# Order of attends, gating products and first loads in a hybrid attention encoder layer

## The chip, the cores and the metric

One core of a Trainium2 chip runs the whole layer. The metric is the device time of one execution in microseconds (us), from the first instruction to the last. The engines are named as the profile names them: PE is TensorE's matrix products and PEld its weight loads, DVE is VectorE, ACT is ScalarE, POOL is GpSimd, SP is SyncE, whose queue issues most of the loads.

## The reference

1024 tokens of width 1024 pass one layer: an attention mixer of four heads and a spatial gating mixer of four groups side by side, an output projection, and an MLP of width 4096, which the change doesn't touch. Cut to the mixers:

```python
h = rmsnorm(x, norm_mix_g)
q, k, v, g, a_f, a_b, su, sv = split(h @ w_in)
# attention, per head, 16 chunks n of 64 tokens, forward scan and mirrored backward scan
b = cumsum(log_a, within the chunk)
scores = mask(q*exp(b - b_mid) @ (k*exp(b_mid - b)).T)
kv[n] = (k*exp(b_last - b)).T @ v
s[n+1] = exp(b_last)[n] * s[n] + kv[n]
o = scores @ v + (q*exp(b)) @ s[n]
o = rmsnorm(o_fwd + o_bwd) * gla_norm_g * silu(g)
# spatial gating, per group of 128 channels, 8 chunks of 128 tokens
v = rmsnorm(gelu(sv)) * sgu_norm_g
out = gelu(su) * (w_s @ v + b_s)
x = x + concat([attention, gating]) @ w_out
x = x + square(relu(rmsnorm(x) @ w1)) @ w2
```

## The kernel before, in words

**Products.** Every operand of a large product is split into a high part (a cast on ACT, L124) and a low part (the difference, on DVE, L125), and each product is three matmuls: high by high, high by low, low by high, all at L106 in `mm`. They add up in PSUM banks: four of the kind `pf` for the projections and four of the kind `pg`, taken in turn, for everything small. A product that takes a bank waits until what was in it has been read.

**The start.** ACT's queue loads the first half of the input's first block, SP's queue the first block of the weights of V (L182, a tile `wr`), then the 24 column vectors of norms (L183, `cols`, 12 KB), then the rest of the inputs `xT` (L194) and the weights `wv` (L135). ACT scales the input by a column of `cols` into `xa` (L186), DVE makes its low part `xb` (L187), and casts (L185) and subtracts (L190) the first weights. The V projection then runs over eight blocks of K, 24 matmuls each.

**The stream.** `stream` (L554) yields 64 steps. Each step is some twelve matmuls of a projection (q, k, attention gate, gating u) or a part of the gating's v. Between the steps lie small pieces of attention and gating, listed in `ev` by hand with the step after which each is issued (L570 to L583). PE executes in the order in which the program is written (`mm` and `transp` keep it, L103 to L110); the other engines' order is set by the scheduler of the framework.

**The pieces.** `u = 2h + hf` numbers head h and half hf of the tokens. For each there are `gate` (decay logarithms `la`, L338), `st_cum` (sums over the chunk, L359), `st_score` (scores and masked copies into `P`, L391, L403), `st_tr` (transposition `kd`, L408) and `st_kv` (L416). `st_kv` fills the states `X[h]`, 16 slots of 128. Its lower 64 partitions are the forward scan, upward from slot 1 (L438). The upper 64 are the backward scan, which runs only when both halves are there, from slot 14 down to slot 0: 14 steps at L444, each of which reads the slot above it. `st_attend` (L449) adds up, in one bank, four products of V and P and eight of X and `qd`: half hf reads the slots 8 hf to 8 hf + 7. Its squares go through ACT (L466), POOL (L211, L212) and DVE (L468). `st_out` (L471) transposes the result, and DVE multiplies it by a column of `cols` and by the head's gate (L476), which the projection of step 39 or 40 (27, 28; 51, 52; 63, 64) leaves.

**Spatial gating.** `sgu_v(hf)` makes one half's v, which POOL scales at its end (L517). `sgu_mix(hf, g)` (L522) is one set of four products for half hf and group g, in a bank that DVE evacuates into `SV` (L526). The names in the trace are `pg<-k,V` for such a set, since `cws` and `cbs` lie in buffers of kind k and SV in one of kind V, and `pg<-V,P`, `pg<-X,qd` and `pg<-ident,kd` for an attend's two parts and a transposition.

The lines that the change and the prediction turn on:

```python
b1 = 7 + 6 * (2 * h + 1) + 11
ev.append((b1 + hf, st_attend, h, hf))
ev.append((b1 + 4 + hf, st_out, h, hf))
```

`b1` is 24, 36, 48 and 60 for the four heads.

Of the kernel before, what the change touches and what calls it, by code (L numbers as in the profile page):

```python
# [31 lines left out]
def tile_encoder(  # L32
# [25 lines left out]
    nc = tc.nc  # L58
# [6 lines left out]
    def sb(tag, bufs, shape=(P, 512), dt=F32):  # L65
        cnt[0] += 1
        home = tiny if tag in ("sm", "rso", "r3") else pool
        return home.tile(list(shape), dt, tag=tag, bufs=bufs, name=f"{tag}{cnt[0]}")

    def one(name, shape, dt=F32):  # L70
        return tiny.tile(list(shape), dt, tag=name, bufs=1, name=name)
# [7 lines left out]
    def in_table_order(ins):  # L79

        if table["last"] is not None:
            tc.add_manual_dep(
                ins.ins,
                table["last"].ins.name,
                mybir.DependencyInfo(mybir.DependencyClass.NoSync, mybir.DependencyReason.DATA),
                reason="table order",
            )
        table["last"] = ins
# [11 lines left out]
    def pg():  # L100
        return bank("pg")

    def mm(o, lhsT, rhs, start, stop, more=False):  # L103

        tc.keep_in_program_order(
            nc.tensor.matmul(out=o, lhsT=lhsT, rhs=rhs, start=start, stop=stop, skip_group_check=more)  # L106
        )
# [4 lines left out]
    def v3(ap, a):  # L112
        return ap.rearrange("p (a b) -> p a b", a=a)

    def bcast_in(ap, n):
        return ap[:, None, :].broadcast_to([ap.shape[0], n, ap.shape[1]])
# [5 lines left out]
    def split(src, hi, lo, scale=None):  # L122
        if scale is None:
            nc.scalar.copy(out=hi, in_=src)  # L124
            return nc.vector.tensor_tensor(out=lo, in0=src, in1=hi.bitcast(F32), op=ALU.subtract)  # L125
        else:
            nc.scalar.activation(out=hi, in_=src, func=AF.Copy, scale=scale)
            nc.vector.scalar_tensor_tensor(
                out=lo, in0=src, scalar=scale, in1=hi.bitcast(F32), op0=ALU.mult, op1=ALU.subtract
            )  # L130

    def wpiece(src):
        with tc.high_priority(offset=HP):
            raw = sb("wr", 2)
            nc.sync.dma_start(out=raw, in_=src)  # L135
            hi, lo = sb("wh", 3, dt=F32R), sb("wl", 3, dt=F32R)
            split(raw, hi, lo)
        return hi, lo
# [3 lines left out]
    ccols = one("cols", [P, 24])  # L142
# [12 lines left out]
    def in_order(ins, after):  # L155
        if after is not None:
            tc.add_manual_dep(
                ins.ins,
                after.ins.name,
                mybir.DependencyInfo(mybir.DependencyClass.NoSync, mybir.DependencyReason.DATA),  # L160
                reason="order of use",
            )
        return ins

    for k in range(KT):
        for hf in range(2):
            raw = sb("qk", 8)
            a, b = sb("xa", 16, dt=F32R), sb("xb", 16, dt=F32R)
            g = ccols[:, G1 + k : G1 + k + 1]
            xh[k, hf], xl[k, hf] = a, b  # L170
            if k == 0 and hf == 0:
                wraw = sb("wr", 2)
                whi, wlo = sb("wh", 3, dt=F32R), sb("wl", 3, dt=F32R)
                h0, h1 = slice(0, 256), slice(256, 512)
                with tc.high_priority(offset=1000):
                    first = nc.scalar.dma_start(out=raw[:, h0], in_=xT[0, :, h0])
                    table["last"] = in_order(
                        nc.scalar.preload_act_table_set("natural_log_exp_and_others"), first
                    )
                    table["logexp"] = True  # L180
                    in_table_order(nc.scalar.copy(out=one("wact", [P, 8]), in_=warm[:, 0:8]))
                    lead = nc.sync.dma_start(out=wraw, in_=wv[0])  # L182
                    lead = in_order(nc.sync.dma_start(out=ccols, in_=cols), lead)  # L183
                    lead = in_order(nc.sync.dma_start(out=raw[:, h1], in_=xT[0, :, h1]), lead)
                nc.vector.tensor_copy(out=whi, in_=wraw)  # L185
                in_table_order(nc.scalar.activation(out=a[:, h0], in_=raw[:, h0], func=AF.Copy, scale=g))  # L186
                nc.vector.scalar_tensor_tensor(  # L187
                    out=b[:, h0], in0=raw[:, h0], scalar=g, in1=a[:, h0].bitcast(F32), op0=ALU.mult, op1=ALU.subtract
                )
                nc.vector.tensor_tensor(out=wlo, in0=wraw, in1=whi.bitcast(F32), op=ALU.subtract)  # L190
                split(raw[:, h1], a[:, h1], b[:, h1], g)
                wvp.append((whi, wlo))
            else:
                nc.sync.dma_start(out=raw, in_=xT[k, :, hf * 512 : hf * 512 + 512])  # L194
                split(raw, a, b, g)
                if hf == 0:
                    wvp.append(wpiece(wv[k]))
# [324 lines left out]
    def sgu_mix(hf, g):  # L522
        mx = pg()
        for i in range(4):
            mm(mx[:, i * P : i * P + P], SV[:, hf * 4 + i, g, :], cws[:, g * P : g * P + P], True, True)
        nc.vector.scalar_tensor_tensor(  # L526
            out=SV[:, hf * 4 : hf * 4 + 4, g, :], in0=v3(mx, 4), scalar=ccols[:, GS + g : GS + g + 1],
            in1=bcast_in(cbs[:, g * P : g * P + P], 4), op0=ALU.mult, op1=ALU.add,
        )
# [40 lines left out]
    ev = []  # L570
    for h in range(H):
        for hf in range(2):
            u = 2 * h + hf
            b0 = 7 + 6 * u
            for off, fn in ((-3 if u == 2 else -4, gate), (0, st_cum), (4, st_score), (5, st_tr), (7, st_kv)):
                ev.append((b0 + off, fn, h, hf))
            b1 = 7 + 6 * (2 * h + 1) + 11
            ev.append((b1 + hf, st_attend, h, hf))
            ev.append((b1 + 4 + hf, st_out, h, hf))
    for g in range(4):  # L580
        ev.append((21 + g, lambda hf, g: sgu_mix(hf, g), 0, g))
        ev.append((41 + g, lambda hf, g: sgu_mix(hf, g), 1, g))
    ev.sort(key=lambda e: e[0])  # L583
    pos = 0
    for _ in stream():
        pos += 1
        while ev and ev[0][0] <= pos:
            _, fn, h, hf = ev.pop(0)
# [553 lines left out]
```

## Time and profile before

| | |
|---|---|
| Runs shown | 1019.97, 1015.92, 1019.59 us; median 1019.59 |
| The profiled execution | 1017.8 us, its span 1016.0 us |
| Granted PE clock, mean | 0.995 |
| Busy | PE 98%, DVE 68%, ACT 47%, POOL 9% |
| Chain that ended last | PE 92%, DVE 5%, ACT 1%, DMA 1% |
| Read from memory, written | 106.77 MB, 37.75 MB |

The profile is one execution. A busy share is that of the whole span; a row of the timeline has the start of an instruction, or of a few alike in a row, their time together, and in brackets the idle time of the engine before them and who ended it. The granted clock is a share of PE's full speed. The stream of 64 steps with attention and gating lies between about 50 and 310 us; what follows is the output projection and the MLP.

### The profile page before, as it was taken

Reading aid. Unit: us, or ns where it says so; the run is one execution under the profiler, and the core shown is the slowest. Engines: PE = TensorE matmul, PEld = TensorE weight load, DVE = VectorE, ACT = ScalarE, POOL = GpSimd, SP = SyncE. Lnnn points to the kernel's source line nnn. Section 1 sums busy time; section 2 is a strip of 40 time slices with the busy share of each in tenths; the row PEclk is TensorE's granted clock in tenths of the full one; section 3 lists DMA queues with packets and bytes.
Section 4 is the critical chain, followed back from the end, with each engine's and each line's share of the span. In section 5 each row is a group of like instructions: output and inputs, shape, how many; then the busy total and the mean of one; then the engine's idle time right before and its main releaser. Section 6 shows DMA issues by size and latency. Waiting matters only on the chain.

```text
span 1016.0 us, 14249 instructions
## 1 busy us (share of the span) xinstructions
PE 1000.5 (98%) x5014; PEld 825.1 (81%) x5014; DVE 693.0 (68%) x1178; ACT 474.0 (47%) x887; POOL 92.6 (9%) x101
## 2 busy tenths in 40 slices
PE   9999999898999999999999999999999999999997
PEld 7887888787888888888888888887888888788885
DVE  6245877776684557877677677665446776799684
ACT  6634646664464446434444433333444444445463
POOL 1001521342220000000000000000000000004031
PEclk9999999999999999999999999999999999999999
DMA  9422111110113444646446445226975652367342
GB/s 307 163 72 74 42 33 63 42 38 26 54 42 123 136 125 134 208 155 218 146 176 214 150 154 177 104 96 232 362 264 178 206 193 69 111 246 263 104 145 83
DMA packets 84984, 145.46 MB, mean 143 GB/s; under 512 B 8881, under 2 KB 17841, under 8 KB 84913
## 3 DMA queue, kind: packets, MB, share of 16 engines
q1 hardware_dynamic: 83760, 142.59, 41.8%
q10 hardware_dynamic: 1152, 1.97, 0.5%
q8 instruction: 39, 0.64, 0.3%
q14 instruction: 33, 0.26, 0.1%
HBM read 106.77 MB, written 37.75 MB: 142 GB/s over the span
## 4 chain that ended last, share of the span: by engine, by line
PE 92%; DVE 5%; ACT 1%; DMA 1%; issue 1%; SPq 0%; POOL 0%; POOLq 0%; DVEq 0%; ACTq 0%
PE pf L106 64%; PE pg L106 27%; PE pg L110 1%; DVE X L444 1%; DVE wl L125 1%; DVE X L438 1%; DMA k<-w 0%; DVE P L403 0%; DMA cols<-cols 0%; DMA wr<-wsv 0%; DVE qk L329 0%; DVE la L343 0%; DVE wl L628 0%; ACT wh L124 0%; DVE kin L382 0%
## 5 line engine op out<-in xcount | busy, mean ns | idle before, releaser
L106 PE MATMUL pg<-xa,xa 128*128 128x512 f32 x768 | 182.5, 390 | 0.4 <-DVE wh L628 0.2
L106 PEld LDWEIGHTS pg<-xa,xa 128*128 128x128 f32 x768 | 144.1, 188 | 31.0 <-DVE wh L628 0.7
L106 PE MATMUL pf<-xa,xa 128*128 128x512 f32 x576 | 138.8, 390 | 0.4 <-ACT kn L792 0.4
L106 PE MATMUL pf<-xa,wh 128*128 128x512 f32 x336 | 136.0, 405 | 0.0
L106 PE MATMUL pf<-xb,wh 128*128 128x512 f32 x336 | 131.9, 392 | 0.0
L106 PEld LDWEIGHTS pf<-xa,xa 128*128 128x128 f32 x576 | 108.0, 188 | 23.3 <-ACT kn L792 0.8
L106 PE MATMUL pf<-xa,wl 128*128 128x512 f32 x320 | 125.6, 393 | 0.0
L124 ACT CAST xa<-xb 128x512 fp32r<-128x512 f32 x76 | 47.1, 621 | 98.2 <-PE pf L106 74.8
L106 PE MATMUL pf<-V,xa 128*128 128x512 f32 x336 | 91.7, 389 | 0.0
L125 DVE TENSOR_TENSOR xa<-xb,xa 128x512 fp32r<-128x512 f32 x76 | 52.3, 689 | 52.8 <-ACT xa L124 52.6
L125 DVE TENSOR_TENSOR wl<-wr,wh 128x512 fp32r<-128x512 f32 x63 | 49.9, 793 | 50.1 <-ACT wh L124 49.8
L106 PEld LDWEIGHTS pf<-xa,wh 128*128 128x128 f32 x336 | 63.9, 190 | 13.9 <-issue 1.2
L941 POOL TENSOR_SCALAR r<-r 128x1 f32<-128x1 f32 x8 | 14.9, 1868 | 657.5 <-ACT tmp L939 657.3
L106 PEld LDWEIGHTS pf<-V,xa 128*128 128x128 f32 x336 | 63.1, 188 | 13.1
L106 PEld LDWEIGHTS pf<-xb,wh 128*128 128x128 f32 x336 | 63.8, 190 | 11.9
L106 PEld LDWEIGHTS pf<-xa,wl 128*128 128x128 f32 x320 | 60.5, 189 | 13.0
L124 ACT CAST wh<-wr 128x512 fp32r<-128x512 f32 x63 | 38.7, 615 | 63.6 <-PE pf L106 54.1
L124 ACT CAST xa<-k 128x512 fp32r<-128x512 f32 x49 | 30.5, 623 | 68.4 <-PE pf L106 66.4
L106 PE MATMUL pf<-xb,xa 128*128 128x512 f32 x192 | 53.9, 389 | 0.0
L106 PE MATMUL pf<-qk,xa 128*128 128x512 f32 x176 | 52.9, 390 | 0.0
L124 ACT CAST xa<-la 128x512 fp32r<-128x512 f32 x34 | 21.1, 622 | 46.5 <-PE pf L106 27.5
L106 PEld LDWEIGHTS pf<-xb,xa 128*128 128x128 f32 x192 | 36.1, 188 | 7.4
(296 smaller groups left out, 1840.4 us busy)
## 6 DMA issues: line engine op xcount, KB each, us to landing
k<-w SPq DMA_DIRECT2D x64, 256.0 KB, 3.1
hA<-kn SPq DMA_DIRECT2D x32, 256.0 KB, 3.1
hS<-wr SPq DMA_DIRECT2D x32, 256.0 KB, 4.3
la<-hA SPq DMA_DIRECT2D x17, 256.0 KB, 5.1
la<-hS SPq DMA_DIRECT2D x17, 256.0 KB, 2.7
qk<-xn SPq DMA_DIRECT2D x16, 256.0 KB, 5.5
wr<-wsv SPq DMA_DIRECT2D x16, 256.0 KB, 2.6
wr<-wo SPq DMA_DIRECT2D x16, 256.0 KB, 2.6
```

Of the source, the lines that this page charges most:

```text
L106: nc.tensor.matmul(out=o, lhsT=lhsT, rhs=rhs, start=start, stop=stop, skip_group_check=more)
L110: tc.keep_in_program_order(nc.tensor.transpose(out=o, in_=i, identity=cid))
L124: nc.scalar.copy(out=hi, in_=src)
L125: return nc.vector.tensor_tensor(out=lo, in0=src, in1=hi.bitcast(F32), op=ALU.subtract)
L438: nc.vector.scalar_tensor_tensor(out=x[lo64, n + 1, :], in0=x[lo64, n, :], scalar=sm[lo64, 2, i : i + 1], in1=v3(kv[i % 2], 4)[lo64, i // ...
L444: nc.vector.scalar_tensor_tensor(out=x[hi64, n - 1, :], in0=x[hi64, n, :], scalar=dec[h, n // 8][hi64, 2, n % 8 : n % 8 + 1], in1=x[hi64, ...
L941: nc.gpsimd.tensor_scalar(out=r[:, 4:5], in0=r[:, 0:1], scalar1=EPS, scalar2=None, op0=ALU.add)
```

## The change

Three edits. The attends and outputs of each head change places: the second half of the tokens first, the first half one step later. The first half's gating products go nine steps later, from the steps 21 to 24 to the steps 30 to 33, and the second half's one step later, from 41 to 44 to 42 to 45. The column vectors are loaded ahead of the first weights.

```diff
-                    lead = nc.sync.dma_start(out=wraw, in_=wv[0])
-                    lead = in_order(nc.sync.dma_start(out=ccols, in_=cols), lead)
+                    lead = nc.sync.dma_start(out=ccols, in_=cols)
+                    lead = in_order(nc.sync.dma_start(out=wraw, in_=wv[0]), lead)
                     lead = in_order(nc.sync.dma_start(out=raw[:, h1], in_=xT[0, :, h1]), lead)
...
             b1 = 7 + 6 * (2 * h + 1) + 11
-            ev.append((b1 + hf, st_attend, h, hf))
-            ev.append((b1 + 4 + hf, st_out, h, hf))
+
+            ev.append((b1 + 1 - hf, st_attend, h, hf))
+            ev.append((b1 + 5 - hf, st_out, h, hf))
     for g in range(4):
-        ev.append((21 + g, lambda hf, g: sgu_mix(hf, g), 0, g))
-        ev.append((41 + g, lambda hf, g: sgu_mix(hf, g), 1, g))
+        ev.append((30 + g, lambda hf, g: sgu_mix(hf, g), 0, g))
+        ev.append((42 + g, lambda hf, g: sgu_mix(hf, g), 1, g))
```

The order on PE at the attends of head 1, steps 36 and 37, before (`P_1293` and `qd_1159` are the first half's, `P_1576` and `qd_1443` the second's):

```order
L106 MATMUL pg_1841<-V_490,P_1293 128x128 x4
L106 MATMUL pg_1841<-X_1457,qd_1159 64x128 x8
L110 MATMUL pg_1863<-ident,kd_1655 128x128 x4
...
L106 MATMUL pg_1890<-V_490,P_1576 128x128 x4
L106 MATMUL pg_1890<-X_1457,qd_1443 64x128 x8
```

And in the change, where `P_1552` and `qd_1419` are the second half's, `P_1281` and `qd_1159` the first's:

```order
L106 MATMUL pg_1841<-V_490,P_1552 128x128 x4
L106 MATMUL pg_1841<-X_1433,qd_1419 64x128 x8
L110 MATMUL pg_1863<-ident,kd_1637 128x128 x4
...
L106 MATMUL pg_1890<-V_490,P_1281 128x128 x4
L106 MATMUL pg_1890<-X_1433,qd_1159 64x128 x8
```

The places on PE are the same; the halves have changed places in them. The dots stand for twelve products of a projection.

The order on DVE over the second part of head 1's scans, before (`sm_1427` holds the second half's decays, `sm_1143` the first's; the sixth backward step is the one ahead of L350):

```order
L438 SCALAR_TENSOR_TENSOR X_1457<-X_1457,sm_1427,pg_1678 64x128
L343 TENSOR_TENSOR la_1733<-pg_1728,k_515 128x512
L444 SCALAR_TENSOR_TENSOR X_1457<-X_1457,sm_1427 64x128
L125 TENSOR_TENSOR wl_1804<-wr_1801,wh_1803 128x512
L438 SCALAR_TENSOR_TENSOR X_1457<-X_1457,sm_1427,pg_1677 64x128
L347 TENSOR_SCALAR tmp_1735<-la_1733 128x512
L444 SCALAR_TENSOR_TENSOR X_1457<-X_1457,sm_1427 64x128
L350 TENSOR_SCALAR la_1733<-la_1733 128x512
```

In the change, the same stretch:

```order
L444 SCALAR_TENSOR_TENSOR X_1433<-X_1433,sm_1403 64x128
L343 TENSOR_TENSOR la_1727<-pg_1722,k_515 128x512
L438 SCALAR_TENSOR_TENSOR X_1433<-X_1433,sm_1403,pg_1665 64x128
L125 TENSOR_TENSOR wl_1804<-wr_1801,wh_1803 128x512
L444 SCALAR_TENSOR_TENSOR X_1433<-X_1433,sm_1403 64x128
L526 SCALAR_TENSOR_TENSOR V_579<-pg_1735,cols,k_577 128x4x128
L347 TENSOR_SCALAR tmp_1729<-la_1727 128x512
L444 SCALAR_TENSOR_TENSOR X_1433<-X_1433,sm_1403 64x128
L350 TENSOR_SCALAR la_1727<-la_1727 128x512
```

The fourth set's evacuation (L526) has come in behind the sixth backward step, ahead of the eight that are left. The third's lies behind the scan's first forward step, the first two's ahead of the scan; the two mask copies of the next half's scores, which lay between the last backward steps, come behind the last one.

The first loads on SP's queue, the difference (`wr_78`, `wr_106`, `wr_124` are the first three pieces of V's weights, the `qk` tiles pieces of the input):

```order
-L182 DMA wr_78<-wv 128x512
-L183 DMA cols<-cols 128x24
+L182 DMA cols<-cols 128x24
+L183 DMA wr_78<-wv 128x512
 L184 DMA qk_75<-xT 128x256
 L135 DMA wr_106<-wv 128x512
 L194 DMA qk_94<-xT 128x512
 L194 DMA qk_100<-xT 128x512
-L135 DMA wr_124<-wv 128x512
 L194 DMA qk_112<-xT 128x512
 L194 DMA qk_118<-xT 128x512
 L194 DMA qk_130<-xT 128x512
+L135 DMA wr_124<-wv 128x512
```

The column vectors go ahead of the first weights, and the third piece of the weights behind three more pieces of the input.

## Rows read from the trace of the kernel before

**Rows 1.** The page, busy us, share of the span, instructions of each engine.

```profile
PE 1000.5 (98%) x5014; PEld 825.1 (81%) x5014; DVE 693.0 (68%) x1178; ACT 474.0 (47%) x887; POOL 92.6 (9%) x101
```

**Rows 2.** Waits of PE, whole span: us in total, times, longest us.

```profile
PE pg L106 <- DVE X L444: 5.5, 2, 2.9
...
PE pg L106 <- DVE la L343: 0.6, 1, 0.6
```

**Rows 3.** PE's timeline at head 0: start us, us, instruction.

```profile
130.53 1.16 PE L106 MATMUL pg<-k,V 128*128 128x128 f32 x8 [0.58 <-DVE la L343]
...
138.75 1.05 PE L106 MATMUL pg<-V,P 128*128 128x128 f32 x8
139.73 1.09 PE L106 MATMUL pg<-X,qd 128*64 128x128 f32 x16
...
141.25 1.06 PE L106 MATMUL pg<-k,V 128*128 128x128 f32 x8
142.06 0.48 PE L106 MATMUL pf<-xa,wh 128*128 128x512 f32 x1
...
144.89 1.05 PE L106 MATMUL pg<-V,P 128*128 128x128 f32 x8
```

**Rows 4.** PE's timeline at head 1's attends.

```profile
185.77 1.05 PE L106 MATMUL pg<-V,P 128*128 128x128 f32 x8
189.47 1.50 PE L106 MATMUL pg<-X,qd 128*64 128x128 f32 x16 [2.65 <-DVE X L444]
...
195.31 1.05 PE L106 MATMUL pg<-V,P 128*128 128x128 f32 x8
```

**Rows 5.** PE's timeline at head 2's attends.

```profile
239.77 1.05 PE L106 MATMUL pg<-V,P 128*128 128x128 f32 x8
...
249.55 1.05 PE L106 MATMUL pg<-V,P 128*128 128x128 f32 x8
```

**Rows 6.** Windows: us, busy PE, PEld, DVE, ACT, POOL, granted clock, DMA, GB/s.

```profile
189.40:192.00 2.60, 2.53 (x21) 2.20 (x22) 2.41 (x5) 2.57 (x8) 0.00 (x0) 0.62 0.00 0
```

**Rows 7.** DVE's timeline in the backward scans of heads 1 and 2.

```profile
181.75 0.35 DVE L444 SCALAR_TENSOR_TENSOR X<-X,sm 64x128 f32<-64x128 f32 x1
...
187.07 0.91 DVE L403 COPY_PREDICATED P<-mkf,pg 64x256 f32<-64x256 uint8 x2
...
189.07 0.35 DVE L444 SCALAR_TENSOR_TENSOR X<-X,sm 64x128 f32<-64x128 f32 x1
...
235.03 0.35 DVE L444 SCALAR_TENSOR_TENSOR X<-X,sm 64x128 f32<-64x128 f32 x1
...
241.06 1.27 DVE L444 SCALAR_TENSOR_TENSOR X<-X,sm 64x128 f32<-64x128 f32 x1
...
243.30 0.35 DVE L444 SCALAR_TENSOR_TENSOR X<-X,sm 64x128 f32<-64x128 f32 x1
```

**Rows 8.** Groups of DVE by line and form, 100 to 320 us: busy, mean ns.

```profile
L526 DVE SCALAR_TENSOR_TENSOR V<-pg,cols,k 128x512 f32<-128x512 f32 x8 | 6.0, 749 | 1.8 <-PE pg L106 1.6
```

**Rows 9.** PE's timeline, the transpositions of steps 30 and 42.

```profile
165.08 0.60 PE L110 MATMUL pg<-ident,kd 128*128 128x128 f32 x4
...
216.40 0.60 PE L110 MATMUL pg<-ident,kd 128*128 128x128 f32 x4
```

**Rows 10.** Timelines of SP, DVE, ACT and PE at the start.

```profile
0.72 0.38 SPq L182 DMA_DIRECT2D wr<-wv  x1
1.16 0.42 SPq L183 DMA_DIRECT2D cols<-cols  x1
...
3.88 0.57 DVE L185 CAST wh<-wr 128x512 fp32r<-128x512 f32 x1 [3.88 <-DMA wr<-wv]
...
4.28 0.51 ACT L186 ACTIVATE xa<-qk,cols 128x256 fp32r<-128x256 f32 x1 [1.63 <-DMA cols<-cols]
...
7.87 0.62 ACT L124 CAST wh<-wr 128x512 fp32r<-128x512 f32 x1
...
5.63 0.52 PE L106 MATMUL pf<-wh,xb 128*128 128x512 f32 x1
```

## The prediction

> **What bounds the kernel now.** I read the shares by engine first: PE is busy in 98% of the span [rows 1], so time can only come from PE's own idle stretches, from slow products, or from fewer products. The change takes no product away, so only the first two are left. Next come PE's waits: two waits on the backward scan X L444, 5.5 us together, and one of 0.6 us on the decay logarithm la L343 [rows 2]. The other waits are in parts that the change doesn't touch, but for the start. Then the order in time around those waits, and the granted clock there.
>
> At head 0, PE goes through the two attends without a wait: first attend at 138.75, its X part at 139.73, the second attend at 144.89 [rows 3]. Between the two lie the X part, a transposition, one spatial-gating product set (141.25 to 142.06, so 0.81 us) and twelve projection products (142.06 to 144.89, 0.236 us each). Without the product set the undisturbed passage is 6.14 - 0.81 = 5.33 us.
>
> Head 1 takes 195.31 - 185.77 = 9.54 us for the same work, with a wait of 2.65 us ahead of the X part [rows 4]. Head 2 takes 249.55 - 239.77 = 9.78 us [rows 5]; its wait is the 2.9 us in [rows 2]. So the loss is **4.21 us at head 1 and 4.45 us at head 2**, some 1.56 us more than the wait in each. The windows say why: the granted clock is 0.62 over the 2.6 us in which head 1's X part and what follows it run [rows 6], between the levels of 1.2 and 2.4 GHz, with PE busy almost all of that time. Head 3 has no such wait.
>
> Why PE waits there: the first half's attend is issued first and reads X[0] to X[7], and the backward scan writes X from index 14 down to 0, so this attend wants the last result of the scan. Head 1's last backward step starts at 189.07, and PE goes on at 189.47 [rows 4, 7]. The second half reads only X[8] to X[15]; the step that writes X[8] is the sixth of fourteen, at 181.75, 7.3 us earlier [rows 7].
>
> **The swap of the attends.** No instruction is added or taken away: the same 4 + 8 + 4 + 8 products per head, with their masks, norms and output transpositions in the other order. What changes is what PE waits for. By itself, on head 1's times of before: X[8] is ready at 182.10, PE's first X part would start at 185.77 + 0.98 = 186.75, and the second attend's X part 5.33 us later, at 192.1, against 189.42 for the whole scan. Both waits go, with 4.6 and 2.7 us to spare.
>
> **The products of spatial gating move into that stretch**, and they work against the swap. The first half's four sets go from steps 21 to 24 to steps 30 to 33, so PE has 4 x 0.81 = 3.24 us more to do ahead of head 1's attend (and as much less earlier, net nothing), and VectorE has four evacuations of 0.75 us [rows 8] more ahead of or inside the scan. I count from the transposition of step 30, 165.08 before [rows 9]:
> - PE reaches the first X part at 185.77 - 165.08 + 0.98 + 3.24 = 24.9, the second attend at 29.2, its X part at 30.2.
> - The scan ended at 189.42 - 165.08 = 24.3. Three sets now lie ahead of the gate products whose result VectorE takes inside the scan: at most 2.43 us. Two of the four evacuations now lie inside the scan, 1.50 us; the other two fit where VectorE idles before it. So it ends by 28.3 at the latest. X[8] comes by 17.0 + 2.43 + 0.75 = 20.2.
> - The second attend takes a bank from which two mask copies (0.91 us, 187.07 [rows 7]) are read, now behind the scan: 28.3 + 0.9 = 29.2, just in time at this upper bound.
>
> Spare: 4.7 us for the first, 1.9 us for the second. At head 2 I count from the transposition of step 42, 216.40 [rows 9]. Only one more set than before lies behind it, the fourth: PE's X parts come at 239.77 - 216.40 + 0.98 + 0.81 = 25.2 and 30.5. The sixth backward step ended at 235.38, so X[8] comes at 19.0 + 0.75, and the whole scan at 27.25 + 0.75 = 28.0 [rows 7]. Spare: 5.4 and 2.5 us. One backward step of this scan took 1.27 us (241.06 [rows 7]), so one more such collision, 0.9 us, would still fit.
>
> By the Trainium skill (SBUF - State Buffer, section "Who interferes with whom"), a VectorE instruction with two SBUF inputs is blocked for the whole of a GpSimd instruction that reads SBUF, while one with at most one such input is not. By that rule the 64 x 128 backward steps can be held up and the four moved evacuations, which read PSUM, can't; the sum stays the same unless three collisions fall in one scan.
>
> At head 0 the la wait of 0.58 us is a wait of the second product set itself, for the bank that the gate's evacuation still reads (130.53 [rows 3]). The set moves away, and the bank's next taker comes a step later. I take 0.58, between 0 (the next taker waits as long) and 0.58.
>
> **New places that could wait.** The two output transpositions swap too. Now the second half's gate (evacuated and sent through ScalarE last) is wanted by the output that VectorE takes first, so its column-scaled write, on which the next transposition's bank depends, comes some microseconds after step 40's products; step 42 lies two steps of twelve products behind, 2 x 2.83 = 5.7 us. I cost it at nothing, and at most at one wait of 1 us. The third and fourth set of head 1 each take a bank from which an earlier set's evacuation must be read; that evacuation now sits behind the scan's first step in VectorE's queue, at most 1 us again.
>
> **The start.** The 12 KB of column vectors are issued first, 0.44 us earlier (0.72 in place of 1.16), the first weights 0.44 us later [rows 10]. Before, the weights' cast started at 3.88 and ScalarE waited for the columns to 4.28. Now ScalarE goes about 0.4 us sooner and the cast later, at 4.3 to 4.9, and VectorE makes the input's low part ahead of the weights' low part, so that the second product (5.63 before) comes at about 5.4. I take -0.2, between -0.44 (the whole shift) and +0.1. The weights of the third piece are also issued after three more input loads. They were cast at 7.87 [rows 10] and are wanted after two pieces of 24 products, 5.63 + 2 x 24 x 0.236 - 0.8 = 16.2, so there are 8 us of cover; without it each late piece would be a PE wait.
>
> **Sum.** 4.21 + 4.45 + 0.58 + 0.2 = 9.4 us. The profiled execution took 1017.8, so 1008.4. The median shown, 1019.59, is 1.8 above that, and the runs go from 1015.92 to 1019.97, so I say **1009**. If the clock part didn't come back (1.56 twice) it would be 3.1 more, 1012.
>
> The Trainium skill (TensorE: Matmul & The Clock Gate, "What's actually happening") holds that half rate is the array's default, released by activity, and that where the change falls differs from run to run. By that rule the clock part goes with the waits, as the trace's undisturbed head 0 has it, but its size would differ from one execution to the next.
>
> **The rivals.**
> 1. *One wait stays or is replaced.* A bank at steps 30 to 42, or head 2's scan with collisions, makes PE wait about 2 to 3 us and run slowly after. That gives back one head's 4.2 to 4.5 us: 1013 to 1014. For it: VectorE's and POOL's queues at the outputs are only a microsecond or two ahead of PE. Against it: the spare times above.
> 2. *The swap doesn't do what it says.* If the attend's first X product waited for the whole of X and not for the slots that it reads, PE would stand at the scan's end as now; the mixed-in sets would only lengthen both sides, 3.24 against up to 3.9. Then 1017 to 1019. Against it: the scan's forward part and PE's reads are already told apart by slot in the program's waits.
> 3. *Slower: the V projection starves.* The third and later weight pieces sit behind more input loads on SP's queue. If they came after 16 us, and each of the six left cost what head 1's wait did (4.21 with the slow restart), that is 25 us: 1008 + 25 = 1033. It outweighs the gain by over 0.5% from the fourth piece on (4 x 4.21 - 9.4 = 7.4 us). Against it: 8 us of cover.
>
> **How the numbers follow.** About 0.5%, 5.1 us, is what a measurement of this kernel tells from no change, so faster means under 1014.5. The forecast has 0.68, rival 1 0.17, rival 2 0.09, rival 3 0.06. Faster: 0.68 and 0.08 of rival 1 make 0.76. Same: the other 0.09 of it and rival 2 make 0.18. Slower: 0.06. The forecast's own range is 1005.5 (9.6 us off the fastest run, a little more at the start) to 1012 (no clock part); with rival 1 it reaches to 1015.
>
> **What the profile afterwards would show.** No PE wait on X L444 in heads 1 and 2, a granted clock of 1.00 through both stretches, some 5.3 us from attend to attend, and 0 to 0.3 us from the start. The la wait at head 0 gone. PE's idle time down by 6.1 us and its slow time by 3.1 us. A row "PE pg <- DVE X L444" of 2 us or more would make rival 2 right; waits on L476, L468 or L526 rival 1; waits on wh L124 or wr in the first 45 us rival 3.

## The result and the profile after

The changed kernel takes **1009.02 us** (median of 6 runs, 1008.54 to 1009.53) against 1019.38 before (6 runs, 1015.92 to 1019.97). The ratio is 0.9905 with a 95% interval from 0.989 to 0.992: 1% faster. The profiled executions compare as 1017.8 with 1008.54, spans 1016.0 and 1006.7, so 9.3 us apart. The medians are 10.4 us apart; the runs of the kernel before lie over 4 us, and an experiment below shows part of the reason in the first 10 us of an execution.

The page after, shares by engine and the chain that ended last:

```profile
PE 997.1 (99%) x5014; PEld 822.4 (82%) x5014; DVE 691.3 (69%) x1178; ACT 475.6 (47%) x887; POOL 93.1 (9%) x101
...
PE 97%; DMA 1%; DVE 1%; ACT 0%; SPq 0%; issue 0%; POOL 0%; POOLq 0%; DVEq 0%
```

DVE had 5% of the chain before and has 1% now, PE 97%. PE has 3.4 us less busy time with the same 5014 products: fewer of them are slow. All waits of PE (us in total, times, longest):

```profile
PE pg L106 <- POOL tmp L147: 1.3, 1, 1.3
PE pf L106 <- ACT kn L793: 0.4, 1, 0.4
PE pf L106 <- DVE xb L128: 0.3, 1, 0.3
PE pg L106 <- DVE wh L629: 0.2, 1, 0.2
PE pg L106 <- DVE wl L629: 0.2, 1, 0.2
```

The two rows of [rows 2], X L444 with 5.5 us and la L343 with 0.6, are gone. A row on xb L128 with 0.3 is new; it is at the start. PE's timeline at the attends of heads 1 and 2, which answers to [rows 4] and [rows 5]:

```profile
185.10 1.05 PE L106 MATMUL pg<-V,P 128*128 128x128 f32 x8
186.08 1.09 PE L106 MATMUL pg<-X,qd 128*64 128x128 f32 x16
...
190.35 1.05 PE L106 MATMUL pg<-V,P 128*128 128x128 f32 x8
...
234.80 1.05 PE L106 MATMUL pg<-V,P 128*128 128x128 f32 x8
235.78 1.09 PE L106 MATMUL pg<-X,qd 128*64 128x128 f32 x16
...
240.05 1.05 PE L106 MATMUL pg<-V,P 128*128 128x128 f32 x8
```

From attend to attend it is now 5.25 us at both heads, against 9.54 and 9.78: 4.29 and 4.53 us less. And DVE's backward scans in the same stretches, for [rows 7]: the sixth step and the last of each head.

```profile
178.18 0.35 DVE L444 SCALAR_TENSOR_TENSOR X<-X,sm 64x128 f32<-64x128 f32 x1
...
185.01 0.35 DVE L444 SCALAR_TENSOR_TENSOR X<-X,sm 64x128 f32<-64x128 f32 x1
...
230.55 0.35 DVE L444 SCALAR_TENSOR_TENSOR X<-X,sm 64x128 f32<-64x128 f32 x1
...
237.33 0.54 DVE L444 SCALAR_TENSOR_TENSOR X<-X,sm 64x128 f32<-64x128 f32 x1
```

Read the two fences against each other. At head 2 the second half's attend starts its X part at 235.78, 1.5 us ahead of the scan's last step, and doesn't wait: it wants X[8], done at 230.90. At head 1 the whole scan is done at 185.36, 0.7 us ahead of the X part. So at head 1 even the old order of the halves would not have waited, because PE comes later there: the experiment with the sets alone tests that. The windows over both stretches (us, then busy PE, PEld, DVE, ACT, POOL, granted clock, DMA share, GB/s), for [rows 6]:

```profile
160.00:200.00 40.00, 40.00 (x301) 33.21 (x300) 32.01 (x72) 22.94 (x50) 11.66 (x14) 1.00 0.21 61
200.00:250.00 50.00, 50.00 (x379) 41.46 (x378) 36.52 (x79) 27.93 (x52) 17.21 (x17) 1.00 0.10 27
```

PE is busy throughout at a granted clock of 1.00, its upper level of 2.4 GHz.

**Where the 9.3 us are.** The same instruction in both timelines gives the account. The end of the V projection, read off the first products behind it, comes 0.2 us later (49.28 against 49.07), the transposition of step 30 4.24 us earlier (160.84 against 165.08). The four sets that left come back between there and head 1's attend: 24.26 us in place of 20.69, so 3.57. Up to here that is 0.7 us less: the la wait gives 0.58, the start takes 0.2, and where the other 0.3 comes from is not traced. Head 1's attends give 4.29, head 2's 4.53. Head 2's second attend stands 9.50 us earlier, and of that 9.3 are left at the end.

### The profile page after: what moved, and what is told of

Same layout as the page of the kernel before. It is cut to its first block, busy times and chain, and to the rows that moved or that the text cites. A ratio compares the mean times of both kernels' runs of the same rounds, so it can differ in the third digit from the quotient of the medians.

```text
span 1006.7 us, 14252 instructions
## 1 busy us (share of the span) xinstructions
PE 997.1 (99%) x5014; PEld 822.4 (82%) x5014; DVE 691.3 (69%) x1178; ACT 475.6 (47%) x887; POOL 93.1 (9%) x101
## 4 chain that ended last, share of the span: by engine, by line
PE 97%; DMA 1%; DVE 1%; ACT 0%; SPq 0%; issue 0%; POOL 0%; POOLq 0%; DVEq 0%
PE pf L106 68%; PE pg L106 28%; PE pg L110 1%; DMA k<-w 0%; DMA wr<-wv 0%; DVE wl L629 0%; ACT xa L124 0%; DVE k L629 0%; DVE xa L125 0%; POOL r L944 0%; DVE xb L128 0%; SPq L827 0%; ACT xa L127 0%; ACT wh L124 0%; DVE wh L629 0%
```

## The experiments

**The swap alone.**

```diff
-            ev.append((b1 + hf, st_attend, h, hf))
-            ev.append((b1 + 4 + hf, st_out, h, hf))
+            ev.append((b1 + 1 - hf, st_attend, h, hf))
+            ev.append((b1 + 5 - hf, st_out, h, hf))
```

> Only the attends and outputs change places; sets and loads as before. Theory A (slots: the second half's attend wants only X[8] to X[15], which the scan has long written): both X waits and their slow stretch go, 8.7 us; the la wait of 0.6 us at head 0 stays; about 1010.6 us against 1019.4, clock 1.00 at both heads. Theory B (what hides the scan is the 3.2 us of product sets moved in front of head 1's attends, the swap alone isn't enough): a wait on X L444 of 1 us or more stays in a head, 1014 us or more.

Measured: 1012.27 us (1011.33 to 1013.23) against 1019.44, ratio 0.9937 [0.9919, 0.9955], span 1009.5. The X waits are gone in every head, and the clock is 1.00 there: theory A's cause holds. But it is 1.7 us above its number, and 2.4 us stand in a wait that I had not expected here. By the spans it is 1016.0 - 1009.5 = 6.5 us, about the 8.8 of the two heads less this wait. Its rows of waits, of PE's timeline and of DVE's:

```profile
PE pg L106 <- DVE V L476: 2.4, 1, 2.4
...
207.78 0.69 PE L106 MATMUL pg<-qin,kin 64*64 64x64 f32 x32
210.89 1.13 PE L106 MATMUL pg<-k,V 128*128 128x128 f32 x8 [2.42 <-DVE V L476]
...
209.99 1.41 DVE L476 SCALAR_TENSOR_TENSOR V<-pg,cols,sg 128x512 f32<-128x512 f32 x2 [1.25 <-ACT sg L95]
```

The set of step 41 takes the bank of the output of step 40. That is the second half's now, and its gate comes last out of ScalarE, so both L476 stand behind it. The change puts this set at step 42.

**The swap with only the second half's sets one step later.**

```diff
-        ev.append((41 + g, lambda hf, g: sgu_mix(hf, g), 1, g))
+        ev.append((42 + g, lambda hf, g: sgu_mix(hf, g), 1, g))
```

> The swap with the second half's sets one step later (42 to 45), the first half's sets at 21 to 24 as before, old order of loads. Theory A (the 2.4 us wait on L476 that the swap alone had is the set of step 41, which takes the bank of the swapped output; one step later it is free): no wait on L476, la wait of 0.6 us stays, 1012.3 - 2.4 = 1009.9 us. Theory B (the first half's sets at 30 to 33 are what hides it): the wait stays above 1 us, 1011.5 us or more.

Measured: 1010.76 us (1008.87 to 1010.79) against 1018.69, ratio 0.9919 [0.9904, 0.9934], span of the profiled execution 1007.1. No wait on L476; the la wait of 0.6 us stays. The span is 2.4 us under the swap's alone, just the wait. So **the move by one step is what keeps the swapped outputs from costing 2.4 us**. What the move by nine steps adds to that is small: this profile's span is 0.4 us above the changed kernel's, which has its la wait gone and its loads in the other order.

**The sets alone.** (Both lines of `sgu_mix` as in the change, the rest as before.)

> Only the sets of spatial gating move; attends in the old order. Theory A (in the changed kernel head 1's whole scan ended 24.5 us after step 30's transposition, and PE reached the X part at 25.2, so there the sets alone suffice; at head 2 the scan ended at 27.3 against 25.2): no wait at head 1, about 2.1 us and a slow stretch of some 1.5 us at head 2; 1019.4 - 4.3 - 0.9 - 0.9 = 1013.3 us (1012 to 1015). Theory B (the swap is needed at both heads, the sets only lengthen the scan as much as PE's work): waits of 2 us or more at both heads, 1018 us or more.

Measured: 1013.24 us (1012.88 to 1013.63) against 1019.44, ratio 0.9946 [0.9931, 0.9962], span 1011.3. The number is theory A's to 0.1 us, but by chance. Its waits and PE's timeline at heads 0 and 2:

```profile
PE pg L106 <- DVE X L444: 3.2, 2, 1.8
...
137.35 1.05 PE L106 MATMUL pg<-V,P 128*128 128x128 f32 x8
140.22 1.09 PE L106 MATMUL pg<-X,qd 128*64 128x128 f32 x16 [1.82 <-DVE X L444]
...
144.50 1.05 PE L106 MATMUL pg<-V,P 128*128 128x128 f32 x8
...
241.04 1.09 PE L106 MATMUL pg<-X,qd 128*64 128x128 f32 x16 [1.35 <-DVE X L444]
```

Head 1 has no wait, as theory A has it. Head 2 waits 1.35 us, less than the 2.1 expected, and without the slow stretch: from attend to attend it is 238.65 to 245.32, 6.67 us, which is about 5.25 plus the wait. But head 0, from which the sets went away, now waits 1.82 us. And this profile's start was the slow one: the transposition that stands at 114.50 before stands at 116.67. So the sets alone move the wait from head 1 to head 0, and of the two edits only the swap takes it from all three heads: **the first half's sets hide the scan at the head that they stand ahead of, head 0 before and head 1 here**.

**Is the slow stretch the idle time's doing?** The kernel before, with needless products where PE would wait:

```diff
         po = pg()
+        if h in (1, 2) and hf == 0:
+            for _ in range(10):
+                mm(po, xh[0, 0][:, :P], xh[0, 0], True, True)
```

> The kernel before, with ten needless products of 128 x 512 ahead of the first half's attend at heads 1 and 2 (some 2.3 us of PE each, into the bank that the attend then starts afresh): PE works where it would idle, and the attend gets no earlier. Theory A (1.56 us of each head's loss is the slow clock that follows the idle stretch): the waits shrink to some 0.4 and 0.6 us, the clock stays at 1.00, attend to attend 5.25 us plus fill and rest of the wait, some 8.1 us in place of 9.54 and 9.78; 3 us faster than before, about 1016.3 us. Theory B (the slow products have another cause, the whole loss hangs on when X is there): 1019.4 us, the clock below 1.00 as before.

Measured: 1014.49 us (1014.28 to 1016.17) against 1018.69, ratio 0.9965 [0.9952, 0.9977], span 1012.6. Twenty products more, and the kernel is 3.4 us faster by the spans. PE's timeline at head 1:

```profile
188.06 1.05 PE L106 MATMUL pg<-V,P 128*128 128x128 f32 x8
189.33 1.09 PE L106 MATMUL pg<-X,qd 128*64 128x128 f32 x16 [0.22 <-DVE X L444]
190.36 0.66 PE L110 MATMUL pg<-ident,kd 128*128 128x128 f32 x4
...
193.61 1.05 PE L106 MATMUL pg<-V,P 128*128 128x128 f32 x8
```

At head 2, and the window over head 1 (columns as for [rows 6]):

```profile
242.03 1.09 PE L106 MATMUL pg<-X,qd 128*64 128x128 f32 x16 [0.66 <-DVE X L444]
...
246.33 1.05 PE L106 MATMUL pg<-V,P 128*128 128x128 f32 x8
...
189.00:193.00 4.00, 3.78 (x31) 3.12 (x31) 3.43 (x7) 3.97 (x13) 0.71 (x2) 1.00 0.15 39
```

The X part of head 1 starts 0.14 us earlier than at 189.47 [rows 4], yet the second attend comes 1.70 us earlier: the X part takes 1.09 and the transposition 0.66, and the granted clock is 1.00 from 189 to 193. Head 2 gives 1.52 us more. From the start of the X part to the second attend it is 4.28 and 4.30 us, where the kernel before takes 5.84 at both heads. Theory A holds: of the 4.2 to 4.5 us per head, 1.56 and 1.54 were the clock.

**The old order, one step later.**

```diff
-            ev.append((b1 + hf, st_attend, h, hf))
-            ev.append((b1 + 4 + hf, st_out, h, hf))
+            ev.append((b1 + 1 + hf, st_attend, h, hf))
+            ev.append((b1 + 5 + hf, st_out, h, hf))
```

> The kernel before, with all attends and outputs one step later, first half still first. Theory A (the loss is only that PE arrives 2.65 and 2.89 us early; a step's twelve products are 2.83): no wait or under 0.2 us on X L444, clock 1.00; about 8.5 us less, 1011 us, as the la wait stays. Theory B (the order of the halves is what counts, or attends that are later push waits into the outputs and the next head's banks): waits of 2 us or more elsewhere, 1013 us or more.

Measured: 1009.31 us (1008.88 to 1012.2) against 1018.69, ratio 0.9915 [0.9897, 0.9933], span 1007.4. No wait on X; two small new ones:

```profile
PE pg L106 <- DVE P L403: 0.3, 1, 0.3
PE pf L106 <- ACT V L95: 0.3, 1, 0.3
```

Theory A: by the spans it is 8.6 us less, where it said 8.5; the median's further distance lies in how the runs of the two kernels are spread. So the order of the halves isn't needed for the gain: what counts is that what PE wants is written before PE gets there, by an earlier result or a later want.

**The loads alone.**

```diff
-                    lead = nc.sync.dma_start(out=wraw, in_=wv[0])
-                    lead = in_order(nc.sync.dma_start(out=ccols, in_=cols), lead)
+                    lead = nc.sync.dma_start(out=ccols, in_=cols)
+                    lead = in_order(nc.sync.dma_start(out=wraw, in_=wv[0]), lead)
```

> Only the column vectors go first. Theory A (the V projection gains 0.46 us at its second product and gives back more in its first block, where inputs land later because more of them are issued at once): second product at about 5.2 us, a wait on xb L128 of 0.3 us, the projection's end 0.2 us later than before, 1019.6 us. Theory B (the start gives 0.2 us as forecast, and the 0.2 us lost in the changed kernel's profile was chance): 1019.2 us, the projection's end 0.2 us earlier.

Measured: 1017.8 us (1016.02 to 1019.33, 10 runs) against 1019.44, ratio 0.999 [0.9979, 1.0002]: not to be told from no change. The profile ends the V projection 0.3 us later (49.38), as theory A has it, but not for the reason that it gives: the second product comes at 5.41 in place of 5.2, the two products at 5.41 and 5.83 have 0.43 us to the next, and no wait on xb L128 is listed.

**The change without the loads,** swap and sets with the old order of loads, in two jobs:

> The change without the loads' order. Theory A (the loads cost 0.2 us): 1008.8 us, the V projection ends as before, all waits on X L444 and la L343 gone. Theory B (the loads help): 1009.3 us or more.

Measured: 1008.75 us (1007.59, 1007.73, 1009.78, 1010.17) against 1019.44, ratio 0.9903 [0.9884, 0.9922].

> The swap and the sets with the old order of loads once more, in more rounds. Four times before gave 1007.6, 1007.7, 1009.8 and 1010.2, and the profile of the last had products 0.43 us apart until 10 us from the start, where the kernel before's profile has 0.23. Theory A (the start has two ways of going, 2.1 us apart, by when the clock rises there): times in two groups, near 1007.7 and 1009.9, none between. Theory B (one spread): times all over 1007.6 to 1010.2.

Measured: 1009.66 us (1007.75, 1008.18, 1009.56, 1009.76, 1010.23, 1010.44) against 1017.67, ratio 0.9918 [0.9903, 0.9933]. No run lies between 1008.2 and 1009.5. PE's timeline at the start of the first job's profiled execution, 1010.17 us:

```profile
5.63 0.80 PE L106 MATMUL pf<-wh,xb 128*128 128x512 f32 x1
6.22 0.63 PE L106 MATMUL pg<-wh,xa 128*128 128x512 f32 x1
...
9.63 0.63 PE L106 MATMUL pf<-wl,xa 128*128 128x512 f32 x1
10.06 0.49 PE L106 MATMUL pg<-wl,xa 128*128 128x512 f32 x1
```

The products follow each other by 0.43 us until 10.06, and by 0.23 after; in the profile before they do so by 0.23 from 5.98 on. Ten or eleven products, 0.2 us each: the 2.1 us between the groups.

That the start has only two ways isn't shown. In the fourteen profiles behind this document the spacing of 0.43 us ends between 5.4 and 6.4 us from the start in ten, at 7.3 in one (the last variant below) and between 9.6 and 10.4 in three; in this second job's own profile, of 1009.56 us, it ends at 9.61. And in the kernel before a second thing varies. Its 40 runs beside the experiments lie at 1015.52 to 1016.34 and 1017.54 to 1018.32 us where the mean granted clock is 0.997, and at 1017.1 to 1017.86 and 1019.19 to 1020.19 where it is 0.994 or 0.995 (one of 0.996 is 1018.69). The 1.7 us between the two clocks are about what the slow stretch of one head costs, 1.56; that nine of the 40 had one slow stretch less is the likely reading, but no profile of such a run was kept. So the median before depends on which of these has more runs, and so does a difference of medians. The 9.3 us of the two profiled executions hold for quick starts, and for a kernel before with both slow stretches.

**The start, held in order.** The changed kernel, with each input and weight load tied behind the one that it followed before, from SP's fourth load on, and the four loads of constants behind them. The loop that does it, without the lines that collect the loads:

```diff
...
+    for key in ((1, "w"), (0, 1), (1, 0), (2, "w"), (1, 1), (2, 0), (2, 1), (3, "w"),
+                (3, 0), (3, 1), (4, 0), (4, 1), (4, "w"), (5, 0), (5, 1), (6, 0)):
+        lead = in_order(seq[key], lead)
...
```

> The changed kernel with the column vectors first, the inputs' and weights' loads held to the order of before. Theory A (the 0.66 us that the changed kernel gave back in its first block came from three more inputs issued ahead of the third weights): no wait on xb L128, the V projection ends 0.4 us earlier than in the kernel before (at 48.6), a time of 1008.3 us. Theory B (the first block is held up by the later first weights themselves): the projection ends at 49.1 to 49.3, 1009.0 us.

Measured: 1008.08 us (1007.55 to 1008.25) against 1017.67, ratio 0.9905 [0.989, 0.992]. The time is theory A's, the profile theory B's: the projection ends at 49.18, and a wait of 0.17 us on xb L128 is left. Which of them holds stays open.

**The start, warmed earlier.** Swap and sets with the old loads:

```diff
-    nc.gpsimd.memset(warm, 0.0)
+    nc.gpsimd.memset(warm[:, :P], 0.0)
+    nc.vector.memset(warm[:, P:], 0.0)
     wps = pg()
-    for n in (512, 256, 128):
+    for n in (128, 128, 256, 512):
```

> Swap and sets, old order of loads, and the needless products at the very start begin earlier: their tile is cleared in two pieces on two engines, and they are 1024 columns in place of 896. Theory A (the slow start comes where PE worked too little ahead of the first product): PE starts at about 0.9 us in place of 1.3, the group at 1009.9 is gone or rare, median 1007.7 us. Theory B (when the clock rises doesn't hang on that): both groups as in the kernel without this, median anywhere between 1007.7 and 1009.9.

Measured: 1007.78 us (1007.5, 1007.72, 1007.74, 1007.83, 1008.81, 1010.27) against 1017.67, ratio 0.9909 [0.9893, 0.9926]. PE starts at 0.98. The median is theory A's; one run in six still lies in the upper group and one between, at 1008.81, where the kernel without this had four in six in the upper group. For so few runs that is a hint and no proof.

**Both, beside the changed kernel on one chip.**

> The changed kernel with the held order of loads and with the earlier needless products. Theory A (the two add up: the loads keep the second product at 5.3, the earlier PE work makes the slow start rare): 1007.5 us median, spread under 1 us, at least 1 us under the changed kernel on the same chip. Theory B (both do the same thing, or the differences of 0.5 to 1 us seen so far were between chips): within 0.5 us of the changed kernel.

Measured: 1007.97 us (1007.83 to 1008.55) against 1017.84, ratio 0.9905 [0.9888, 0.9921].

> The changed kernel itself, beside the last variant on the same chip. Theory A: 1009.0 us as before, between the two groups that the old order of loads gives. Theory B (its 1009.0 was that chip's): within 0.5 us of the other variant.

Measured: 1009.18 us (1008.66 to 1009.27) against 1017.84, ratio 0.9914 [0.99, 0.9929]. The variant is 1.2 us below the changed kernel, and their runs don't overlap. That is theory A's distance, at a median 0.5 above its number, and a tenth of a per cent. Its way there isn't shown: in the variant's profile the second product comes at 5.60, not 5.3, and the products are 0.43 us apart until 7.26. Each of the two parts had about as low a median without the other, 1008.08 and 1007.78 on another chip, so which of them gives the 1.2 us stays open. PE's timeline in this execution of the changed kernel shows what its order of loads can cost:

```profile
8.23 0.40 PE L106 MATMUL pg<-wl,xa 128*128 128x512 f32 x1
9.22 0.50 PE L106 MATMUL pf<-wh,xa 128*128 128x512 f32 x1 [0.59 <-ACT xa L127]
10.01 0.50 PE L106 MATMUL pf<-wh,xb 128*128 128x512 f32 x1 [0.28 <-DVE xb L128]
```

Twelve products in, at the second half of the first block, PE waits for the input's second piece, 0.87 us in all; in the first profile of the same kernel it was 0.29. The variant has no such wait, and its projection ends at 49.65 where this one's ends at 50.74.

## Why the prediction was right, and where it wasn't

- **What bounds the kernel; the loss per head.** Right. Forecast 4.21 and 4.45 us, measured 4.29 and 4.53; the undisturbed passage is 5.25 where I had 5.33. The split into wait and clock, 2.65 and 1.56 at head 1, is shown by the needless products: from the X part to the second attend 1.56 and 1.54 us came back at the two heads.
- **The swap.** Right in its cause: the X part of head 2 runs ahead of the scan's last step. Rival 2 is out by that row.
- **The sets in head 1's stretch.** Forecast for PE 24.9, 29.2 and 30.2 us after step 30's transposition, measured 25.2, 29.5 and 30.5. For X[8] I had 20.2 at the latest and measured 17.7; for the whole scan 28.3 and 24.5. The bounds held, and were wide. VectorE over the scan, before and after (us, busy and instructions, granted clock, DMA share, GB/s), and what comes behind the scan's last step now:

```profile
175.63:189.42 13.79, 12.88 (x33) 1.00 0.25 78
171.70:185.36 13.66, 12.74 (x30) 1.00 0.21 58
...
185.40 0.92 DVE L403 COPY_PREDICATED P<-mkf,pg 64x256 f32<-64x256 uint8 x2
186.35 0.93 DVE L403 COPY_PREDICATED P<-mkb,pg 64x256 f32<-64x256 uint8 x2
```

  The scan had no more idle time to give than it has now, 0.9 us. Two evacuations came into it, 1.5 us, and four mask copies, 1.8 us, went out behind it. I added the first and didn't take off the second. Nor did the 2.43 us of sets ahead of the gate products hold the scan: one more backward step runs ahead of the gate's result. So head 1 had 6.0 us to spare where I said 1.9, and the old order would have done.
- **Head 2.** Forecast 25.2 and 30.5 for PE, measured 25.25 and 30.5; X[8] 19.75 against 20.4, the scan 28.0 against 27.3. One collision falls into this scan, as before, and a shorter one. Its last backward step takes 0.54 us beside a product on GpSimd:

```profile
236.44 1.28 POOL L548 TENSOR_TENSOR V<-V,sg 128x512 f32<-128x512 f32 x1 [11.92 <-ACT sg L95]
```

  The step ends 0.15 us behind that product, as the one of 1.27 us did before (242.33, behind a product from 240.92 to 242.18). So 3.2 us were to spare where I said 2.5.
- **Head 0.** The la wait went, as forecast. That the sets had also been hiding the scan at head 0 I did not see: without the swap they leave a wait of 1.82 us there.
- **New places that could wait.** I cost the swapped outputs at nothing, since step 42 lies 5.7 us behind them. The second L476 of head 1 ended at 209.49 and the set came at 210.97: 1.5 us to spare. One step earlier it would have cost 2.4. The step holds; its margin was smaller than my words made it.
- **The start.** Wrong in sign, by 0.4 us. "The second product comes at about 5.4": it came at 5.17, 0.46 earlier than before. The step that failed is that this stays gained: the term came to +0.2 where I bounded it by -0.44 and +0.1. PE's timeline after:

```profile
5.17 0.45 PE L106 MATMUL pf<-wh,xb 128*128 128x512 f32 x1
...
8.56 0.50 PE L106 MATMUL pf<-wh,xb 128*128 128x512 f32 x1 [0.29 <-DVE xb L128]
...
49.28 1.95 PE L106 MATMUL pg<-ident,rs 128*128 128x128 f32 x16
```

  The input's second piece lands later, 4.4 us behind its issue in place of 3.9, and the projection ends 0.2 us later than before (49.07). I looked for the cost at the third weights, which had 8 us of cover (cast at 10.53, wanted at 16.2, so rival 3 is out), and not at the second input. Nor is the 0.46 steady: in the other executions with the columns first the second product came at 5.34 to 5.60. It was the smallest term, and didn't move the sum.
- **The sum.** Forecast 9.4 us off the profiled execution, measured 9.26. The median of 1009.02 beside the forecast 1009 owes its last digits to chance: the median before leaned towards the slow start, and I had set the figure between the two ways of counting. By the Trainium skill (TensorE: Matmul & The Clock Gate, "What's actually happening") the default is half rate, released by activity. The trace agrees at the attends: no idle stretch is left there, and the granted clock is 1.00, against 0.62 and 0.71 behind the idle stretches before. That the size of the clock part would differ from one execution to the next no profile shows: in the two kept ones with both waits, before and with the loads alone, the X part and what follows it take 5.84 and 5.84, and 5.81 and 5.87 us to the second attend. The run times of the kernel before hint at it, as said above.

## What to carry to other kernels

When an engine waits for the last result of a serial chain, ask which consumer needs the early results and let it go first, or issue the whole consumer one step later: here each removed the wait, and a wait of 2.7 us gave back 4.3, as the slow products behind it went too. A reordering shifts which result comes last on the engines behind it, so the next taker of a bank may have to move along; the swap without the one-step move lost 2.4 us at such a bank. And work that is moved into a stretch to hide a chain is missing where it came from.

## What the runs showed of the hardware

- Behind the waits of 2.65 and 2.89 us PE's granted clock fell to 0.62 [rows 6] and 0.71 over the next 2.4 to 2.6 us, between 1.2 and 2.4 GHz. Behind those of 1.35, 1.82 and 2.42 us in the variants it stayed at 1.00, and the products kept their usual length. Head 2 before, then the windows behind 1.82 us (sets alone) and 2.42 us (swap alone):

```profile
243.71 1.13 PE L106 MATMUL pg<-X,qd 128*64 128x128 f32 x16 [2.89 <-DVE X L444]
243.60:246.00 2.40, 2.29 (x21) 2.08 (x22) 1.79 (x4) 1.09 (x2) 0.40 (x1) 0.71 0.00 0
...
140.20:142.70 2.50, 2.48 (x25) 2.13 (x26) 1.57 (x3) 1.33 (x9) 0.10 (x1) 1.00 0.00 0
...
210.80:213.40 2.60, 2.51 (x15) 2.29 (x16) 2.47 (x6) 0.00 (x0) 0.00 (x0) 1.00 0.00 0
```

- The start differs from run to run in one and the same kernel, by up to 2.1 us: the products go over from 0.43 to 0.23 us apart somewhere between 5.4 and 10.4 us. From 5.5 to 10.0 us 11 products ran in one profile and 20 in another, and the granted clock in the records is 1.00 in both, so there the spacing of the products is the thing to read, not the clock column.
- Needless products in front of a wait can pay: twenty of them made the kernel before 0.35% faster.
